# Prefix-sum diagonal on one core: more groups summed over rows by VectorE before TensorE, one row more per strip for ScalarE

## The chip, the core and the metric

The kernel runs on one core of a Trainium2 chip. A core has TensorE (PE, matrix products into PSUM), VectorE (DVE), ScalarE (ACT), GpSimd (POOL), SyncE (SP), and 16 DMA engines that bring data from the device memory to the on-chip memory of 128 partitions. The metric is device time in microseconds (us): 667.77 us, the median of 3 runs (667.74 to 668.14). One further execution was recorded by the profiler; the trace is of that one.

## What is computed

The input is x, four matrices of 4224 x 4224 float32 values (285 MB). For each matrix the result is the running sum along the diagonal of its two-dimensional prefix sums:

```python
ps = np.cumsum(np.cumsum(x, axis=1), axis=2)
diag = np.diagonal(ps, axis1=1, axis2=2)
return np.cumsum(diag, axis=1).astype(np.float32)
```

The diagonal entry n is the sum of the square x[0..n, 0..n]. So step n of it adds column n down to row n (above and on the diagonal) and row n up to column n-1 (left of the diagonal). The kernel forms these two sums for every n, adds them, and scans twice.

## The kernel before

A batch (one matrix) is cut along rows into strips. A strip has 768 rows, held as 128 partitions of F2 = 6 consecutive rows each, all 4224 columns wide, converted to bf16 by the DMA. There are NS = 5 such strips (s = 0 to 4) and then one of F = 3 rows per partition (384 rows). Columns are counted in NG = 11 groups of GW = 384. The last batch has four strips of 768 rows (s = 0 to 3), then one tile filled by two half-strip transfers of three rows per partition each (called the first and second half here), and the last 128 rows of the matrix are a tail of their own with `part_a` and `part_b`.

Three buffers hold strips (`NBUF` = 3). Strip DMAs are issued by POOL in program order (`load_rows`, line 75). The first three are issued at the start; each later one waits until everything that reads its buffer (the strip three places earlier) is done.

For each strip, `add_up` does the following.

- TensorE sums columns: for each group j to the right of the strip's own diagonal block, and for each of the six rows q, one matmul of 384 columns adds the strip into row j of `d`, an 11 x 384 accumulator in PSUM (`columns`; line 218 for the first of six, line 225 for the others).
- VectorE splits the diagonal block: `mu` is the block times an upper-triangular mask (line 353), and `mu` is subtracted from the block in place (line 354).
- In the first three batches, for strips s > 0, VectorE also adds the six rows of one group, the one just right of the block, into `rowed` (`row_sums`, line 267). TensorE then needs one fp32 matmul (run as two instructions) for this group in place of six.
- TensorE adds `mu` to `d`, two groups of six matmuls, and then `rowed`.
- The row sums left of the diagonal: ScalarE sums rows 0 to fs-1 of each partition, one activation with an accumulator per row (`act_sum`, line 262); VectorE sums the remaining rows in one reduction (line 267, `acc`). For 768-row strips fs = F = 3, so three rows each. Both read columns 0 to `hi`, the end of the strip's block: 768, 1536, 2304, 3072 and 3840 columns for s = 0 to 4.

After the strips of a batch VectorE copies the row sums to `r6` (line 400), TensorE adds them to `d`, VectorE makes sums of `d` (`pu`), TensorE forms the carries between groups, and VectorE scans twice (line 479).

Each engine works through its own instructions in program order. In the last batch this order is, for VectorE: strip s = 3 (`mu`, subtraction, `acc`), the two copies of line 400, the first half of the half strips (`mu`, subtraction, one row sum of 3456 columns), the second half, the fold of `fold_g`, the last row sums, `pu`, the scans, and the pair sums of the tail. For TensorE: the columns and `mu` of s = 3, six matmuls and three `mu` matmuls of the first half, 28 matmuls into a scratch tile called `ready` whose result is not used, 12 matmuls of `fold_g` over the second half (these use the PSUM buffer of `ready`), six more of the second half, the additions of the row sums to `d`, the folds `fold_part(0)` and `(1)`, the carries, and the tail with `fin_a`, `fin_b`, `fin_e`. The result `ye` is copied by VectorE and sent by SP as the last transfer.

The small pools matter for the order: `mu` and `rowed` come from `mup`, which has one buffer per name, so that each is written again only after TensorE has read it.

Of the kernel before, what the change touches and what calls it, by code (L numbers as in the profile page):

```python
# [8 lines left out]
FP32 = mybir.dt.float32  # L9
# [4 lines left out]
ACT = mybir.ActivationFunctionType  # L14
# [3 lines left out]
def kernel(  # L18
# [14 lines left out]
    nc = tc.nc  # L33
# [3 lines left out]
    P = 128  # L37
    F = 3
    F2 = 2 * F
    GW = P * F  # L40
    NG = N // GW
# [9 lines left out]
    mup = ctx.enter_context(tc.tile_pool(name="mup", bufs=1))  # L51
# [18 lines left out]
    def strip_tile():  # L70
        return strips.tile([P, F2, N], BF16, name="strip")

    def load_rows(o, b, r0):
        f = o.shape[1]
        nc.gpsimd.dma_start(  # L75
            out=o, in_=x[b, r0 : r0 + f * P, :].rearrange("(p f) w -> p f w", f=f)
        )
# [16 lines left out]
    sel = consts.tile([P, 2 * NG - 1], BF16, name="sel")  # L94
# [3 lines left out]
    def upper_mask(f):  # L98

        um = consts.tile([P, f, f * P], BF16, name=f"um{f}")  # L100
        nc.vector.memset(um, 1.0)  # L101
        nc.gpsimd.affine_select(  # L102
            out=um,
            in_=um,
            compare_op=ALU.is_gt,
            fill=0.0,
            base=0,
            pattern=[[-1, f], [1, f * P]],
            channel_multiplier=-f,
        )  # L110
        return um

    sel_f = consts.tile([P, 2 * NG - 1], FP32, name="sel_f")
    nc.vector.tensor_copy(out=sel_f, in_=sel)

    um6 = upper_mask(F2)
    um3 = upper_mask(F)
# [3 lines left out]
        out=um1,  # L121
        in_=um1,
# [10 lines left out]
        out=ident,  # L133
        in_=ident,
# [32 lines left out]
    def between_groups(name, turned):  # L167
# [27 lines left out]
        out=weights,  # L195
        in_=weights,
# [12 lines left out]
        out=steps, in_=steps, scalar=2, op=ALU.arith_shift_right  # L209
# [7 lines left out]
    def matmul(o, lhsT, rhs, start=False):  # L217
        nc.tensor.matmul(  # L218
            o, lhsT=lhsT, rhs=rhs, start=start, stop=False, skip_group_check=True
        )  # L220
# [36 lines left out]
    def act_sum(acc, src, own=None):  # L257
        w = src.shape[-1]
        dump = own
        if dump is None:  # L260
            dump = src
        nc.scalar.activation(  # L262
            out=dump[:, :w], in_=src, func=ACT.Copy, accum_out=acc
        )

    def row_sums(acc, src):
        nc.vector.reduce_sum(out=acc, in_=src, axis=AX.X)  # L267
# [18 lines left out]
    def masked(o, i, m, acc):  # L286
        nc.vector.scalar_tensor_tensor(  # L287
            out=o,
            in0=i,
            scalar=1.0,  # L290
            in1=m,
            op0=ALU.mult,
            op1=ALU.mult,
            accum_out=acc,
        )
# [21 lines left out]
    for b in range(B):  # L317
        whole = b < LB
        t0 = 0 if whole else 1
        r6, r3 = rows6[b % 2], rows3[b % 2]  # L320
        d = psum_d.tile([NG, GW], FP32, name="d")
# [6 lines left out]
        def row_of(j):  # L328
            return (j + t0) % NG

        def columns(j, lo, hi, rhs, same=False):


            k = row_of(j)
            lhsT = sel[:, NG - 1 - k : 2 * NG - 1 - k]
            if same:
                matmul_on(d[:, lo:hi], lhsT, rhs)
                return
            matmul(d[:, lo:hi], lhsT, rhs, start=first[0])
            first[0] = False  # L340

        def add_up(strip, f, r0, acc, um, fs=0, wp=0, ws=0, by_rows=False):


            nw = f * P // GW
            g = r0 // GW
            hi = r0 + f * P
            for j in range(g + nw + by_rows, NG):
                for q in range(f):
                    columns(j, 0, GW, strip[:, q, j * GW : (j + 1) * GW], q > 0)  # L350
            mu = mup.tile([P, f, f * P], BF16, name=f"mu{f}")
            block = strip[:, :, r0:hi]
            nc.vector.tensor_mul(out=mu, in0=block, in1=um)  # L353
            nc.vector.tensor_sub(out=block, in0=block, in1=mu)  # L354
            if by_rows:
                rowed = mup.tile([P, GW], FP32, name="rowed")
                row_sums(
                    rowed,
                    strip[:, :, hi : hi + GW].rearrange("p q c -> p c q"),
                )  # L360
            for h in range(nw):
                for q in range(f):
                    columns(g + h, 0, GW, mu[:, q, h * GW : (h + 1) * GW], q > 0)
            if by_rows:
                k = row_of(g + nw)
                matmul(d, sel_f[:, NG - 1 - k : 2 * NG - 1 - k], rowed)
            if fs:
                for q in range(fs):
                    act_sum(acc[:, q : q + 1], strip[:, q, :hi])
                row_sums(acc[:, fs:], strip[:, fs:, :hi])  # L370
            else:
                for q in range(f):
                    act_sum(acc[:, q, 0:1], strip[:, q, wp:ws])
                row_sums(acc[:, :, 1], strip[:, :, ws:hi])

        acc6 = smalls.tile([P, NS, F2], FP32, name="acc6")

        ns = NS if whole else NS - 1
        for s in range(ns):
            strip = prefetched.pop(0) if prefetched else None  # L380
            if strip is None:
                strip = strip_tile()
                load_rows(strip, b, s * F2 * P)
            add_up(
                strip, F2, s * F2 * P, acc6[:, s], um6, F, by_rows=whole and s > 0
            )
            if not whole and s == 0:
                diag_b = last.tile([P, P], BF16, name="diag_b")
                nc.gpsimd.dma_start(out=diag_b, in_=x[b, TB:N, TB:N])
            if not whole and s == 1:  # L390
                row_sums(hs[:, 2:3], diag_b)
                masked(hmu[:, 2, :P], diag_b, um1[:, :P], hu[:, 2:3])
                nc.vector.tensor_sub(out=dtot, in0=hs[:, 2:3], in1=hu[:, 2:3])
                for h in range(3):
                    columns(LG, h * P, GW, hmu[:, h, : GW - h * P], h > 0)
        a6 = acc6[:, :ns]
        for h in range(2):
            ps = slice(h * HP, (h + 1) * HP)
            k = row_of(h)
            nc.vector.tensor_copy(  # L400
                out=r6[ps, k : k + 2 * ns : 2, :], in_=a6[ps]
            )

        strip = strip_tile()
        if whole:
            load_rows(strip[:, :F], b, T0)
            add_up(strip[:, :F], F, T0, r3[:, LG], um3, F - 1)
        else:


            for h in range(2):
                load_rows(strip[:, h * F : h * F + F], b, T0 - (2 - h) * GW)
            add_up(strip[:, :F], F, T0 - 2 * GW, r3[:, row_of(LG - 2)], um3, F - 1)
            ready = psum_s.tile([P, 512], FP32, name="fold")
            for i in range(28):
                matmul(ready, ident_h, um6[:, i % F2, :512], start=True)
            fold_g = psum_s.tile([P, F, 160], FP32, name="fold")
            wp, ws = 1920, 1920 + 1248
            fold_in(fold_g, strip[:, F:], 0, wp, 160, start=True)
            parts = last.tile([P, F, 3], FP32, name="parts")  # L420
            add_up(strip[:, F:], F, T0 - GW, parts, um3, wp=wp, ws=ws)
            row_sums(parts[:, :, 2], fold_g)
            row_sums(r3[:, row_of(LG - 1), :], parts)

        if not whole:

            strip = strip_tile()
# [8 lines left out]
            for sb, c0, c1 in (  # L436
# [6 lines left out]
                r0 = TB + sb * R  # L443
                nc.gpsimd.dma_start(  # L444
                    out=part_b[:, sb, c0:c1],
                    in_=x[b, r0 : r0 + R, :TB].rearrange("r (k c) -> r k c", k=4)[
                        :, :, c0:c1
                    ],
# [3 lines left out]
            c0, c1 = acuts[0]  # L452
# [25 lines left out]
        for i, (to, src) in enumerate(((c1, d), (c2, c1))):  # L478
            nc.vector.tensor_tensor_scan(  # L479
                out=to,  # L480
# [29 lines left out]
        c0, c1 = acuts[1]  # L510
# [24 lines left out]
        for i in (1, 0):  # L535
# [5 lines left out]
            out=out[:LB, :].rearrange("b (g i) -> g b i", i=GW), in_=whole_sums  # L541
        )
        nc.sync.dma_start(
            out=out[b, :T0].rearrange("(g i) -> g i", i=GW), in_=last_sums[1:NG]
        )
        nc.sync.dma_start(
            out=out[b, T0 : T0 + M0].unsqueeze(0), in_=yl[:, :M0]
        )
        for i in (1, 0):
# [8 lines left out]
            out=out[b, T0 + M0 : T0 + E0].unsqueeze(0), in_=yl[:, M0:E0]  # L558
# [35 lines left out]
```

## Time and profile before

| | |
|---|---|
| median of 3 runs | 667.77 us (667.74 to 668.14) |
| profiled execution, its time | 667.48 us |
| profiled execution, span of the trace | 665.4 us |
| DMA queue of the strips, share of 16 engines | 99.9% (142.47 MB) |
| VectorE busy | 334.5 us (50%) |
| TensorE matmuls busy | 211.2 us (32%), 997 instructions |
| ScalarE busy | 154.5 us (23%) |
| GpSimd busy | 31.7 us (5%) |

The span is the time from the first to the last instruction on the core; 2.1 us of the execution's time lie around it. Times inside the trace are counted from the span's start. A line of the timeline gives start, duration, engine, source line, operation, output and inputs, and in brackets the idle time before it and what ended it. In the table of stretches, each engine's busy time and number of instructions are followed by the TensorE clock that was granted (1.00 is full speed, 0.50 half), the busy share of the DMA engines and their rate.

### The profile page before, as it was taken

The page shows a single profiled execution, that of the slowest core. Times are in us where ns is not written, and L with a number is a line of the kernel's source. Part 1 is how long each engine was busy: PE and PEld are TensorE (multiplying, and loading weights), DVE is VectorE, ACT ScalarE, POOL GpSimd, SP SyncE. Part 2 cuts the span into 40 slices and gives each one's busy share as a digit, 9 for nine tenths or more (in the row PEclk, how much of TensorE's full clock was granted, in tenths as well). Part 3 has the DMA queues.
Part 4 walks back from the last instruction along what each step waited for, and adds up shares of the span by engine and source line. Part 5 has one row for each costly group of instructions (what it writes and reads, how often), then busy time and mean ns, then how long its engine had stood idle before and what let it go on. Part 6 is the DMA issues. An engine that isn't in the chain of part 4 may idle for free.

```text
span 665.4 us, 2519 instructions
## 1 busy us (share of the span) xinstructions
PE 211.2 (32%) x997; PEld 97.2 (15%) x998; DVE 334.5 (50%) x160; ACT 154.5 (23%) x145; POOL 31.7 (5%) x60
## 2 busy tenths in 40 slices
PE   0071422303107143230311623404022253250458
PEld 0030210101103021010110311201001121120224
DVE  4141727466914163655782325456487323251746
ACT  0010203133511020322450102123154010221443
POOL 4200000000000000000000000000000000001000
PEclk9995857655558585665555957567565595765789
DMA  9999999999999999999999999999999999999998
GB/s 203 219 219 219 219 219 218 213 213 210 220 219 218 219 219 219 218 215 213 212 220 218 219 216 219 219 218 217 212 216 216 218 218 219 218 218 216 216 205 164
DMA packets 7666, 143.24 MB, mean 215 GB/s; under 512 B 698, under 2 KB 998, under 8 KB 2150
## 3 DMA queue, kind: packets, MB, share of 16 engines
q0 software_dynamic: 7312, 142.47, 99.9%
q1 hardware_dynamic: 342, 0.61, 0.3%
q8 instruction: 8, 0.13, 0.1%
q14 instruction: 4, 0.03, 0.0%
HBM read 285.47 MB, written 0.07 MB: 429 GB/s over the span
## 4 chain that ended last, share of the span: by engine, by line
DVE 42%; another core or an unknown queue 40%; DMA 11%; ACT 3%; issue 1%; PE 1%; POOL 1%; DVEq 0%; ACTq 0%; POOLq 0%
DVE acc L267 19%; DMA strip<-in_x_dram 11%; DVE mu L353 7%; DVE strip L354 7%; DVE rowed L267 7%; ACT strip L262 3%; PE d L218 0%; DVE c L479 0%; DVE whole_sums L479 0%; POOL strip L444 0%; DVE pu L267 0%; DVE whole_sums L287 0%; POOL strip L433 0%; DVE rows L400 0%
## 5 line engine op out<-in xcount | busy, mean ns | idle before, releaser
L262 ACT ACTIVATE strip<-strip 128x768 bf16<-128x768 bf16 (+9 forms) x71 | 150.3, 2118 | 481.7 <-DVE strip L354 450.8
L353 DVE TENSOR_TENSOR mu<-strip,um 128x4608 bf16<-128x4608 bf16 (+1 forms) x24 | 52.4, 2183 | 294.3 <-DMA strip<-in_x_dram 294.2
L225 PEld LDWEIGHTS <-sel 128*11 128x11 bf16 x643 | 66.5, 103 | 475.0 <-issue 445.1
L267 DVE TENSOR_REDUCE acc<-strip 128x3 f32<-128x2304 bf16 (+4 forms) x19 | 134.8, 7094 | 0.2
L218 PE MATMUL d<-strip,sel 128*11 128x384 bf16 x90 | 37.2, 413 | 286.9 <-DMA strip<-in_x_dram 286.9
L225 PE MATMUL d<-strip,sel 128*11 128x384 bf16 x441 | 115.6, 405 | 13.8 <-DMA strip<-in_x_dram 13.8
L354 DVE TENSOR_TENSOR strip<-strip,mu 128x4608 bf16<-128x4608 bf16 (+1 forms) x24 | 52.4, 2183 | 1.5
L267 DVE TENSOR_REDUCE rowed<-strip 128x384 f32<-128x2304 bf16 x12 | 49.3, 4110 | 0.0
L218 PE MATMUL d<-mu,sel 128*11 128x384 bf16 x43 | 15.9, 370 | 103.1 <-DVE mu L353 103.1
L225 PE MATMUL d<-mu,sel 128*11 128x384 bf16 x200 | 45.9, 364 | 0.0
L75 POOL DMA_DIRECT2D strip<-in_x_dram x23 | 15.7, 684 | 534.7 <-DVE acc L267 287.9
L218 PE MATMUL d<-rowed,sel_f 128*11 128x384 f32 x24 | 11.5, 568 | 21.9 <-DVE rowed L267 21.9
L267 DVE TENSOR_REDUCE rows<-strip 128x1 f32<-128x4224 bf16 (+1 forms) x4 | 17.4, 4353 | 0.1
L218 PEld LDWEIGHTS <-sel 128*11 128x11 bf16 x134 | 13.5, 101 | 22.7 <-issue 10.2
L262 ACT ACTIVATION_READ_ACCUMULATOR strip<-strip 128x1 f32 x71 | 13.2, 186 | 0.0
L218 PE MATMUL d<-ident,rows 128*11 128x128 f32 x24 | 5.7, 374 | 16.5 <-ACT strip L262 16.5
L267 DVE TENSOR_REDUCE pu<-d 11x1 f32<-11x384 f32 x4 | 2.2, 545 | 14.1 <-PE d L218 14.1
L218 PE MATMUL fold<-um,ident_h 128*128 128x512 bf16 x27 | 6.3, 392 | 0.3 <-issue 0.3
L262 ACT ACT_TABLE_LOAD x1 | 1.3, 1283 | 19.7 <-DMA strip<-in_x_dram 19.7
L102 POOL TENSOR_SCALAR_AFFINE_SELECT um<-um 128x4608 bf16<-128x4608 bf16 (+1 forms) x2 | 5.2, 2612 | 7.3 <-DVE um L101 7.3
L101 DVE MEMSET um<- 128x4608 bf16 (+1 forms) x2 | 4.9, 2458 | 1.1 <-issue 1.1
L218 PEld LDWEIGHTS d<-rowed,sel_f 128*11 128x11 f32 x24 | 1.5, 91 | 26.8 <-DVE rowed L267 26.4
(114 smaller groups left out, 75.8 us busy)
## 6 DMA issues: line engine op xcount, KB each, us to landing
strip<-in_x_dram POOLq DMA_DIRECT2D x18, 6336.0 KB, 73.5
strip<-in_x_dram POOLq DMA_DIRECT2D x7, 3168.0 KB, 57.5
strip<-in_x_dram POOLq DMA_DIRECT2D x1, 1080.0 KB, 51.6
strip<-in_x_dram POOLq DMA_DIRECT2D x1, 768.0 KB, 54.6
strip<-in_x_dram POOLq DMA_DIRECT2D x3, 256.0 KB, 55.9
head<-in_x_dram SPq DMA_DIRECT2D x1, 528.0 KB, 3.9
strip<-in_x_dram POOLq DMA_DIRECT2D x1, 192.0 KB, 43.2
strip<-in_x_dram POOLq DMA_DIRECT2D x1, 64.0 KB, 28.6
```

The source lines that it names most:

```text
L75: nc.gpsimd.dma_start(out=o, in_=x[b, r0 : r0 + f * P, :].rearrange("(p f) w -> p f w", f=f))
L101: nc.vector.memset(um, 1.0)
L102: nc.gpsimd.affine_select(out=um, in_=um, compare_op=ALU.is_gt, fill=0.0, base=0, pattern=[[-1, f], [1, f * P]], channel_multiplier=-f,)
L218: nc.tensor.matmul(o, lhsT=lhsT, rhs=rhs, start=start, stop=False, skip_group_check=True)
L225: te.add_instruction(mybir.InstMatmult(start_tensor_calc=False, stop_tensor_calc=False, tile_position=(0, 0), tile_size=(P, P if lhsT.shap ...
L262: nc.scalar.activation(out=dump[:, :w], in_=src, func=ACT.Copy, accum_out=acc)
L267: nc.vector.reduce_sum(out=acc, in_=src, axis=AX.X)
L353: nc.vector.tensor_mul(out=mu, in0=block, in1=um)
L354: nc.vector.tensor_sub(out=block, in0=block, in1=mu)
```

## The change

In every 768-row strip of all batches, two (s = 0) or three (other s) groups to the right of the block are first added over their six rows by VectorE, as far as there are that many: for s = 4 one group is left. Before it was one group, for s > 0, in the first three batches only. Each such group has a `rowed` buffer of its own. TensorE drops six bf16 matmuls per group and gets one fp32 matmul. ScalarE takes four of the six row sums to the left of the diagonal (F2 - 2) and VectorE two. A small constant, `sel_f`, is converted by ScalarE and no longer by VectorE.

```diff
     sel_f = consts.tile([P, 2 * NG - 1], FP32, name="sel_f")
-    nc.vector.tensor_copy(out=sel_f, in_=sel)
+    nc.scalar.activation(out=sel_f, in_=sel, func=ACT.Copy)
...
-        def add_up(strip, f, r0, acc, um, fs=0, wp=0, ws=0, by_rows=False):
+        def add_up(strip, f, r0, acc, um, fs=0, wp=0, ws=0, by_rows=0):
...
             block = strip[:, :, r0:hi]
             nc.vector.tensor_mul(out=mu, in0=block, in1=um)
             nc.vector.tensor_sub(out=block, in0=block, in1=mu)
-            if by_rows:
-                rowed = mup.tile([P, GW], FP32, name="rowed")
+            rowed = []
+            for i in range(by_rows):
+                rowed.append(mup.tile([P, GW], FP32, name=f"rowed{i}"))
+                c0 = hi + i * GW
                 row_sums(
-                    rowed,
-                    strip[:, :, hi : hi + GW].rearrange("p q c -> p c q"),
+                    rowed[i],
+                    strip[:, :, c0 : c0 + GW].rearrange("p q c -> p c q"),
                 )
             for h in range(nw):
                 for q in range(f):
                     columns(g + h, 0, GW, mu[:, q, h * GW : (h + 1) * GW], q > 0)
-            if by_rows:
-                k = row_of(g + nw)
-                matmul(d, sel_f[:, NG - 1 - k : 2 * NG - 1 - k], rowed)
+            for i in range(by_rows):
+                k = row_of(g + nw + i)
+                matmul(d, sel_f[:, NG - 1 - k : 2 * NG - 1 - k], rowed[i])
...
             add_up(
-                strip, F2, s * F2 * P, acc6[:, s], um6, F, by_rows=whole and s > 0
+                strip,
+                F2,
+                s * F2 * P,
+                acc6[:, s],
+                um6,
+                F2 - 2,
+                by_rows=min(2 if s == 0 else 3, NG - 2 * s - 2),
             )
```

## The prediction

> **What bounds the kernel now.** I read the page's busy table and its DMA lines first:
>
> ```profile
> PE 211.2 (32%) x997; PEld 97.2 (15%) x998; DVE 334.5 (50%) x160; ACT 154.5 (23%) x145; POOL 31.7 (5%) x60
> ...
> q0 software_dynamic: 7312, 142.47, 99.9%
> ```
>
> No engine is busy for more than half the span, while the strip queue keeps the 16 DMA engines busy for 99.9%. Then I cut the span at the times when strips land (where VectorE's `mu` of each begins):
>
> ```profile
> 34.59:64.54 29.95, 7.67 (x3) 0.77 1.01 217
> 64.54:95.19 30.65, 14.01 (x4) 0.67 0.99 212
> 125.14:155.09 29.95, 18.79 (x4) 0.61 1.01 217
> 589.05:618.90 29.85, 12.47 (x3) 0.61 1.01 217
> ```
>
> A 768-row strip takes 29.9 us whether VectorE works 7.7 or 18.8 us of it. Compute can only matter if it starves this queue, or after the last landings. The end of the chain that ended last shows the second:
>
> ```profile
> 619.15 43.18 DMA strip<-in_x_dram
> 662.35 0.41 DVE pair L276 x2
> 662.76 0.04 issue
> 662.81 0.48 PE fin_e L218 x6
> 663.29 0.02 issue
> 663.31 0.18 DVE ye L562
> ```
>
> The last piece lands at 662.35 and 1.0 us later the result is copied. The stretch before that, in the timeline:
>
> ```profile
> 624.21 9.75 DVE L267 TENSOR_REDUCE acc<-strip 128x3 f32<-128x9216 bf16 x1
> 634.07 0.36 DVE L400 COPY rows<-acc 64x24 f32<-64x24 f32 x2
> 634.46 0.76 DVE L353 TENSOR_TENSOR mu<-strip,um 128x1152 bf16<-128x1152 bf16 x1
> 636.04 3.75 DVE L267 TENSOR_REDUCE rows<-strip 128x1 f32<-128x3456 bf16 x1
> 637.23 6.31 PE L218 MATMUL fold<-um,ident_h 128*128 128x512 bf16 x27 [0.33 <-issue]
> 648.88 0.58 PE L218 MATMUL fold<-strip,ident_h 128*128 128x480 bf16 x1 [5.34 <-DMA strip<-in_x_dram]
> 648.93 0.76 DVE L353 TENSOR_TENSOR mu<-strip,um 128x1152 bf16<-128x1152 bf16 x1 [9.13 <-DMA strip<-in_x_dram]
> 657.66 0.38 PE L218 MATMUL fold_a<-strip,ident_h 128*128 128x512 bf16 x1 [0.29 <-DMA strip<-in_x_dram]
> ```
>
> Before the last half strip lands (648.88), VectorE has idled 9.1 us and TensorE 5.3 us. That idle time is what the change can use up.
>
> **The change, part by part.**
>
> *Whole-span sums.* The `rowed` reductions go from 12 to 47 (12 per whole batch, 11 in the last): 35 x 4.11 us = 144 us on VectorE. Two rows for three saves a third of the 134.8 us of `acc`, 45 us. Net 334.5 + 99 = 433 us, under the span. ScalarE gains 19 activations of 0.83 to 3.39 us, about 41 us. TensorE drops 210 bf16 matmuls and gains 70 fp32 ones.
>
> *Does the queue starve?* A strip's buffer comes free 3 x 4.03 us after the subtraction, not 1 x, less the saved row. VectorE's end moves, for s = 1, 2, 3 of a whole batch, by 8.1 less 1.6, 2.4 and 3.2 us (a third of 4.9, 7.3 and 9.7), so by 6.5 to 4.9 us later; s = 0 moves from 46.5 (TensorE) to 49.8. For s = 4 VectorE ends 4.0 us earlier; ScalarE, with four activations at 3.4 us, takes over the end at about 174.0, still earlier than 176.4. The tightest cover: the issue at 144.71 moves to 149.6, and its strip is next in line only at 170.1 (it lands at 200.1, less 29.9). So 20 us of queued transfers hide it, 25 us or more elsewhere. In the last batch (no `rowed` before, so 12.1 less 1.6 or 2.4 us) the issues of 570.0 and 602.4 move by about 10 us; their data are next at 618.9 and 648.9, 37 us later. All cost nothing. If such cover were gone, each us late would be a us of the span. POOL's issues keep their order. `sel_f`, 21 columns on ScalarE, is done before the first strip lands at 34.6.
>
> *The end of the last batch.* This is where the sum is made.
>
> 1. VectorE, s = 3: 624.21 + 3 x 4.03 + 6.5 (two thirds of 9.75) + 0.1 = 642.9; the copies end at 643.3. The `mu` of the first half starts at 643.3 in place of 634.46: 8.8 us late. It, the subtraction and the 3.75 us reduction end at 648.6, so VectorE is just free (0.3 us) for the last half. Its own delay is hidden; TensorE's is not.
> 2. TensorE, in order: the third `rowed` at 636.4 (1.3 us at half clock), six columns until 639.6, then idle until `mu` at 644.1. The three `mu` matmuls and the gap after them took 1.1 us (635.73 to 636.83), so `ready` begins at 645.2.
> 3. The 28 `ready` matmuls and the 12 of `fold_g` behind them depend on the granted clock. At half clock `fold_g` matmuls of 480 columns start every 0.40 us (weight loads at 649.26, 649.66, 650.06), so those of 512 every 0.427; at full clock it is half of that and a little more, 0.203 and 0.216 (`ready` before: 2.4 slow and 25.6 fast ones and 0.17 us of drain make its 6.7 us). The clock is at half after 4.4 us of idling, as in the trace:
>
> ```profile
> 624.00:626.00 2.00, 2.00 (x13) 0.95 1.06 228
> 637.00:638.00 1.00, 0.77 (x3) 0.57 1.24 270
> 648.00:649.00 1.00, 0.12 (x1) 0.55 1.01 203
> 651.00:652.00 1.00, 1.00 (x6) 0.74 1.06 216
> ```
>
> The means place the rises at 624.2, 637.9 and 651.5: 5.3, 4.0 and 2.6 us after the first matmul (618.90, 633.86, 648.88). With the middle one the clock rises at 648.1: 2.9 us of half clock make 6.8 matmuls, 21.2 more take 4.6 us, and with 0.17 us of drain `ready` ends at 652.85. `fold_g` starts at 652.9, not 648.88, but runs at full clock: 12 x 0.203 = 2.4 us, so the next matmul is at 655.35 instead of 652.70. **2.65 us late.**
> 4. ScalarE is no later: the two 3.08 us rows after 645.0, then the three short ones, end at 655.0, before `fold_g` is reduced.
> 5. The additions to `d`, `pu`, carries and scans follow one another and keep the 2.65 us: the last scan ends at 662.1. Two TensorE waits for DMA (0.29 before 657.66, 0.45 before 659.07) vanish, and the one idle bit before `fin_a` shrinks, so `fin_a` starts at 662.95 (before 660.47). From there TensorE needs 1.9 us to the end of the `bsum` matmuls (before 662.40), 664.9, and `fin_e` follows at once where it waited before for the last pair sum. `ye` is copied at 665.35 instead of 663.31: **2.05 us late.**
>
> With the rise after 2.6 us `ready` ends 0.7 us earlier, after 5.3 us 0.65 us later: 1.4 and 2.7 us. I take the middle row. Sum: 667.48 + 2.05 = **669.5 us**. The profiled execution is 0.29 us under the median of 667.77, which is within the runs' spread (0.40).
>
> The Trainium skill, TensorE: Matmul & The Clock Gate, Part 1, says that the clock is released after a busy window of about 3.4 us, that the windows run freely, and that an idle window takes it back. By it the rise after 644.1 comes 3.4 to 6.8 us later and the end is 1.8 to 3.4 us late, 669.3 to 670.9. The trace disagrees at the short side, where 2.6 us were enough; so a window seems not to need to be busy throughout.
>
> *Costs that the trace does not show.* `rowed` over the second and third group: bound by its own row, 4.08 to 4.18 us each, and by an `acc` of the same 2304 elements, 2.55; I take 4.03 from start to start, as the order of columns is `rowed`'s. A two-row `acc`: between one row (3.75 for 3456 columns) and three (9.75). DMA per strip: 29.85 to 30.65 us; I take no change.
>
> **The rivals.**
>
> *The clock is already full at 644.1.* The new burst of 636.4 to 639.6 might wake it; the clock also stayed full for 4.6 us after a last matmul (643.5 to 648.1), and here 4.4 pass. Against: the burst lasts 3.2 us and the rises took 2.6 to 5.3, and elsewhere the clock fell sooner (at 50.8 after matmuls that end at 47.9). Then `ready` ends at 651.4, `fold_g` follows at full clock, the next matmul comes at 653.9, 1.2 us late, and the end, which returns 0.6 as above, 0.6 us late: 668.1.
>
> *VectorE overruns the last half too.* Its margin is 0.3 us. If `rowed` took 4.6 us beside four ScalarE rows, the first `mu` and all behind it would be 1.7 us later still, and the last `mu` 1.4 us late: 671.2. It decides from 4.13 us on, where the margin is gone (3 x 0.1). Against: 4.08 to 4.18 in all 12.
>
> *Other side: faster.* With less TensorE traffic transfers could run faster. The span is 22 strip times long, and to come out 1.3 us under the median in spite of the late end each would have to shrink by 0.14 us (3.1 us in all); intervals do differ by up to 0.8 us (30.65 and 29.85). At 0.2 us each, 4.4 us: 665.1. Against: 29.95 with TensorE busy for 13.28 us (34.59 to 64.54) and for 6.90 us (125.14 to 155.09) alike.
>
> *The tail hides all* (`ready` never holds up the half strip): 667.5. Against: TensorE's order above.
>
> **How the numbers follow.** A measurement of this kernel can tell about 0.2% (1.3 us) from no change: 666.4 to 669.1 counts as same. The forecast gets 0.74, range 668.8 to 670.3; 0.09 of it lies under 669.1. The clock rival 0.10 (same), the overrun 0.06 (slower), the hidden tail 0.03 (same), faster transfers 0.07. So slower 0.71, same 0.22, faster 0.07. The range reaches to the hidden tail and towards the overrun: 667.4 to 670.8.
>
> **What would show it.** After: strips still land every 29.9 us and the last piece near 662.4; `rowed` x47 at 4.1 us; the first half's `mu` near 643.3; `ready` ending near 652.9 and the first `fold_g` matmul after it, no longer released by DMA; `ye` near 665.3. The prediction is wrong if strip intervals change, if a `mu` waits for something other than its landing in mid-batch, or if `fold_g` still starts at 648.9.

## The result, and the profile after

The changed kernel takes 669.15 us in the median of 22 runs (668.20 to 670.70), the kernel before 667.82 us in 22 runs beside it (667.37 to 668.86). The ratio is 1.0019, with a 95% interval of 1.0013 to 1.0025: slower by 1.3 us. The loss is clear of zero. It lies at the bound of 0.2% that the prediction set for "no change", which the interval includes. The profiled execution took 668.88 us, with a span of 667.2 us; before it was 667.48 and 665.4.

The first lines of the page after:

```profile
PE 222.5 (33%) x858; PEld 82.7 (12%) x858; DVE 428.7 (64%) x194; ACT 193.2 (29%) x184; POOL 31.7 (5%) x60
...
q0 software_dynamic: 7312, 142.47, 99.7%
...
L267 DVE TENSOR_REDUCE rowed<-strip 128x384 f32<-128x2304 bf16 x47 | 189.2, 4078 | 0.0
```

VectorE works 94 us more (prediction: 99), and the strip queue is as full as it was. TensorE has 139 matmul records fewer and is nevertheless "busy" for longer, because the bf16 matmuls that are left run more often at half clock (those on `mu` take 412 ns in the mean, before 364) and the added fp32 ones are slow (705 ns mean). Neither sum says anything about the end time here.

Cutting the span after the change at the landings of strips (columns: stretch, its length, VectorE's busy time and instructions, granted clock, DMA share, GB/s):

```profile
34.62:64.58 29.96, 14.77 (x5) 0.77 1.01 217
64.58:95.42 30.84, 20.32 (x7) 0.67 0.99 212
125.31:155.25 29.94, 23.59 (x7) 0.56 1.01 217
589.12:618.99 29.87, 21.94 (x6) 0.61 1.01 217
```

VectorE's share of these stretches has grown from 7.7 to 14.8 us and from 18.8 to 23.6 us, but the landings keep their distance. The strip s = 3 of the last batch lands at 618.99; before it was 618.95. Up to this point nothing is lost.

The timeline after, from there on, as VectorE and TensorE show it:

```profile
624.13 12.09 DVE L267 TENSOR_REDUCE rowed<-strip 128x384 f32<-128x2304 bf16 x3
636.12 6.56 DVE L267 TENSOR_REDUCE acc<-strip 128x2 f32<-128x6144 bf16 x1
643.17 0.76 DVE L353 TENSOR_TENSOR mu<-strip,um 128x1152 bf16<-128x1152 bf16 x1
648.95 0.76 DVE L353 TENSOR_TENSOR mu<-strip,um 128x1152 bf16<-128x1152 bf16 x1 [0.44 <-DMA strip<-in_x_dram]
655.41 0.66 DVE L267 TENSOR_REDUCE parts<-fold 128x3 f32<-128x480 f32 x1 [2.62 <-PE fold L225]
664.96 0.18 DVE L570 COPY ye<-fin_e 1x32 f32<-1x32 f32 x1 [0.31 <-PE fin_e L218]
```

```profile
643.98 0.48 PE L218 MATMUL d<-mu,sel 128*11 128x384 bf16 x1 [4.34 <-DVE mu L353]
645.03 7.70 PE L218 MATMUL fold<-um,ident_h 128*128 128x512 bf16 x28
652.78 0.36 PE L218 MATMUL fold<-strip,ident_h 128*128 128x480 bf16 x1
655.30 0.33 PE L218 MATMUL d<-strip,sel 128*11 128x384 bf16 x1
```

VectorE itself is in time for the last half strip: it starts at its landing (648.95) after 0.44 us of idling. TensorE is not. Its first `fold_g` matmul has lost the bracket that named the DMA before. It follows the 28 `ready` matmuls directly, 3.9 us after the landing, and VectorE then waits 2.6 us for it. The chain that ended last no longer runs through the last transfer. It goes back through TensorE's `ready` to VectorE's `rowed`:

```profile
624.21 12.00 DVE rowed L267 x3
636.22 6.47 DVE acc L267
642.78 0.17 DVE rows L408
642.96 0.18 DVE rows L408
643.17 0.77 DVE mu L353
643.98 0.48 PE d L218
644.46 0.64 PE d L225 x2
645.10 7.65 PE fold L218 x28
```

### The profile page after: what moved, and what is told of

The parts are those of the page before. It is cut to its first block, busy times and chain, and to the rows that moved or that the text cites. A ratio compares the mean times of both kernels' runs of the same rounds, so it can differ in the third digit from the quotient of the medians.

```text
span 667.2 us, 2307 instructions
## 1 busy us (share of the span) xinstructions
PE 222.5 (33%) x858; PEld 82.7 (12%) x858; DVE 428.7 (64%) x194; ACT 193.2 (29%) x184; POOL 31.7 (5%) x60
## 4 chain that ended last, share of the span: by engine, by line
DVE 54%; another core or an unknown queue 27%; ACT 10%; DMA 5%; PE 3%; issue 1%; POOL 0%; DVEq 0%; ACTq 0%; POOLq 0%
DVE rowed L267 26%; DVE acc L267 10%; ACT strip L262 10%; DVE mu L353 8%; DVE strip L354 8%; DMA strip<-in_x_dram 5%; PE fold L218 1%; PE d L218 1%; DVE c L487 1%; DVE whole_sums L487 0%; PE fold L225 0%; DVE pu L267 0%; DVE whole_sums L287 0%; DVE rows L408 0%
## 5 line engine op out<-in xcount | busy, mean ns | idle before, releaser
L262 ACT ACTIVATE strip<-strip 128x768 bf16<-128x768 bf16 (+8 forms) x90 | 189.0, 2101 | 458.9 <-DVE strip L354 458.9
L267 DVE TENSOR_REDUCE rowed<-strip 128x384 f32<-128x2304 bf16 x47 | 189.2, 4078 | 0.0
L225 PEld LDWEIGHTS <-sel 128*11 128x11 bf16 x468 | 50.7, 108 | 374.2 <-issue 357.0
L218 PE MATMUL d<-rowed,sel_f 128*11 128x384 f32 x94 | 57.3, 705 | 109.3 <-DVE rowed L267 109.3
L267 DVE TENSOR_REDUCE acc<-strip 128x2 f32<-128x1536 bf16 (+4 forms) x19 | 90.8, 4777 | 0.0
L218 PE MATMUL d<-strip,sel 128*11 128x384 bf16 x55 | 23.5, 428 | 167.3 <-DMA strip<-in_x_dram 167.3
L225 PE MATMUL d<-strip,sel 128*11 128x384 bf16 x266 | 73.5, 421 | 13.8 <-DMA strip<-in_x_dram 13.8
L218 PE MATMUL d<-mu,sel 128*11 128x384 bf16 x43 | 17.8, 414 | 130.1 <-DVE mu L353 130.1
L225 PE MATMUL d<-mu,sel 128*11 128x384 bf16 x200 | 53.9, 412 | 0.0
L218 PEld LDWEIGHTS d<-rowed,sel_f 128*11 128x11 f32 x94 | 5.4, 95 | 147.0 <-DVE rowed L267 146.4
L262 ACT ACTIVATION_READ_ACCUMULATOR strip<-strip 128x1 f32 x90 | 16.8, 187 | 0.0
L218 PEld LDWEIGHTS <-sel 128*11 128x11 bf16 x99 | 10.8, 109 | 26.1 <-issue 16.7
L218 PE MATMUL d<-halves,rows 128*11 128x64 f32 x48 | 5.3, 289 | 0.0
```

The lines of the kernel that those rows point to most:

```text
L218: nc.tensor.matmul(o, lhsT=lhsT, rhs=rhs, start=start, stop=False, skip_group_check=True)
L225: te.add_instruction(mybir.InstMatmult(start_tensor_calc=False, stop_tensor_calc=False, tile_position=(0, 0), tile_size=(P, P if lhsT.shap ...
L262: nc.scalar.activation(out=dump[:, :w], in_=src, func=ACT.Copy, accum_out=acc)
```

## Experiments

The theory was that all of the loss arises in this end of the last batch, by TensorE's queue. The main rivals were a loss spread over the batches, a lateness of VectorE and ScalarE themselves, and a clock that is missing when the last half strip lands.

### The one strip undone, and the one strip alone

Undone, from the changed kernel:

```diff
-                by_rows=min(2 if s == 0 else 3, NG - 2 * s - 2),
+                by_rows=0 if not whole and s == 3 else min(2 if s == 0 else 3, NG - 2 * s - 2),
```

> The changed kernel, but strip s = 3 of the last batch has no rowed groups (TensorE adds its three groups column by column, as before); the other 44 rowed groups and ScalarE's fourth row stay. Theory A (the time was lost only in the last batch's end: the first half strip's mu 8.7 us late, and ready and fold_g behind it on TensorE): the first half's mu is back near 631, fold_g starts with the landing at 648.9, ye near 663.3, time as the kernel before, 667.8 (ratio 0.9995 to 1.0005). Rival B (the 1.3 us are spread over the batches: VectorE's 100 us more, later buffers): at least two thirds of the loss stays, 668.7 to 669.1.

Measured: 667.43 us (667.20 to 668.16, 10 runs), ratio 0.9994 (0.9985 to 1.0003). The loss is gone, although 44 of 47 `rowed` groups are still there. The first half's `mu` came at 636.10, not near 631 as expected. The half strip had landed before that, as TensorE's first matmul on it shows (634.17); `mu` had to wait behind VectorE's copies of the row sums, and these waited 4.62 us for ScalarE's fourth row. In this variant the fourth row thus holds up VectorE, which the expectation had left out. It costs nothing, as `fold_g` is released by its DMA again:

```profile
634.17 0.48 PE L218 MATMUL d<-strip,sel 128*11 128x384 bf16 x1 [8.04 <-DMA strip<-in_x_dram]
635.71 0.36 DVE L408 COPY rows<-acc 64x24 f32<-64x24 f32 x2 [4.62 <-ACT strip L262]
636.10 0.76 DVE L353 TENSOR_TENSOR mu<-strip,um 128x1152 bf16<-128x1152 bf16 x1
649.15 0.38 PE L218 MATMUL fold<-strip,ident_h 128*128 128x480 bf16 x1 [3.92 <-DMA strip<-in_x_dram]
663.62 0.18 DVE L570 COPY ye<-fin_e 1x32 f32<-1x32 f32 x1 [0.31 <-PE fin_e L218]
```

Alone, with all other strips as before:

```diff
-                F2 - 2,
-                by_rows=min(2 if s == 0 else 3, NG - 2 * s - 2),
+                F2 - 2 if not whole and s == 3 else F,
+                by_rows=3 if not whole and s == 3 else int(whole and s > 0),
```

> The other way round: all strips as before the change, and only strip s = 3 of the last batch gets its three rowed groups and ScalarE's fourth row. Theory A: 669.1 (ratio 1.0015 to 1.0025), ye near 665.0. Rival B: no more than 668.2, as 44 of 47 rowed groups and most of VectorE's added work are gone.

Measured: 669.30 us (668.37 to 670.35, 10 runs), ratio 1.0022 (1.0013 to 1.0032). One of the 19 strips of 768 rows brings the whole loss. The two together rule out a loss spread over the batches.

### What in that strip's wake is late

The `ready` matmuls write a scratch tile that nobody reads. Their number was cut to 10 in the changed kernel:

```diff
-            for i in range(28):
+            for i in range(10):
                 matmul(ready, ident_h, um6[:, i % F2, :512], start=True)
```

> The changed kernel with 10 scratch matmuls in ready instead of 28; their result is not used. Theory A1 (TensorE's backlog of ready matmuls is what is late): ready ends near 648.7 (at 645.0, seven at half clock and three at full), fold_g starts with the landing at 648.95 at full clock, ye near 663.4, time 667.6 to 667.9. Rival A2 (VectorE's and ScalarE's own lateness carries the delay: ScalarE's short rows end at 654.8 in place of 652.65): the row sums stay late, 668.7 to 669.2. Rival A3 (without ready the clock stays at half through fold_g): next matmul near 653.8, time 668.2.

> The changed kernel with 10 scratch matmuls in ready once more, with more rounds: ratio to the kernel before 0.9990 (0.9985 to 0.9995). If the first result was chance: 1.0000.

Measured: 667.24 us (667.09 to 667.75, 10 runs), ratio 0.9989 (0.9979 to 0.9998), and again 667.27 us (667.08 to 667.55, 11 runs), ratio 0.9989 (0.9980 to 0.9998). The first theory's expectation, 667.6 to 667.9, was nearest; why the time is lower still is taken up below. VectorE's `mu` is as late as in the changed kernel, yet the loss is gone:

```profile
643.14 0.76 DVE L353 TENSOR_TENSOR mu<-strip,um 128x1152 bf16<-128x1152 bf16 x1
645.40 3.21 PE L218 MATMUL fold<-um,ident_h 128*128 128x512 bf16 x9 [0.33 <-issue]
648.87 0.38 PE L218 MATMUL fold<-strip,ident_h 128*128 128x480 bf16 x1 [0.26 <-DMA strip<-in_x_dram]
654.81 0.16 DVE L267 TENSOR_REDUCE rows<-parts 128x3 f32<-128x9 f32 x1 [1.49 <-ACT strip L262]
663.33 0.18 DVE L570 COPY ye<-fin_e 1x32 f32<-1x32 f32 x1 [0.31 <-PE fin_e L218]
```

So the late `mu` does its harm only through the `ready` matmuls queued behind it. ScalarE's lateness is visible too: the `parts` reduction waits 1.49 us for its rows. But its delay of 1.2 us (654.81 against 653.57) is within what the end can absorb: `ye` is copied at 663.33, before the change at 663.31. There is little left to absorb with, for the chain that ended last now runs through `acc`, `mu` and ScalarE's rows and no longer through a transfer.

Without `ready` altogether (the tile and the loop taken out of the changed kernel):

> The changed kernel without ready. TensorE idles from 645.0 to 648.9 after three short matmuls, so fold_g runs at half clock at first. If only TensorE's backlog made the change slow, this is at 667.4 to 667.9, as the kernel before and 0.2 to 0.6 us over the variant with 10. If the clock at the landing were what the change lost, it would be 668.5 or more.

Measured: 667.28 us (667.03 to 668.11, 10 runs), ratio 0.9991 (0.9982 to 1.0000). In its profile 11 of the `fold_g` matmuls take 4.60 us at half clock instead of the 2.39 of the changed kernel:

```profile
649.65 4.60 PE L225 MATMUL fold<-strip,ident_h 128*128 128x480 bf16 x11
```

The chain that ended last runs through them. This execution was the slowest of the ten (668.11 us), so the half clock may well cost something where it occurs; in the median nothing of it is seen.

### How much VectorE time the end can hold

Two groups instead of three in that one strip:

```diff
-                by_rows=min(2 if s == 0 else 3, NG - 2 * s - 2),
+                by_rows=min(2 if s == 0 or not whole and s == 3 else 3, NG - 2 * s - 2),
```

> The changed kernel with two rowed groups, not three, in the last batch's s = 3; all else stays. Theory A1 (TensorE's backlog decides, with a threshold): the first half's mu at 639.2, ready from 640.3 to about 648.3, still before the landing at 648.9, so nothing is lost: 667.3 to 667.6. A theory in which each group costs its share (4 us of VectorE each, a third of the loss): 668.7.

Measured: 667.69 us (667.17 to 668.52, 10 runs), ratio 0.9997 (0.9988 to 1.0006). The cost has a threshold and is not a third per group: two thirds of the loss would have been 668.7. In its profile the `mu` is at 639.78, but `ready` does not end near 648.3 as expected. The clock rose late, and `fold_g` starts at 650.26, 0.7 us after the landing of that execution:

```profile
642.04 8.16 PE L218 MATMUL fold<-um,ident_h 128*128 128x512 bf16 x27 [0.33 <-issue]
650.26 0.36 PE L218 MATMUL fold<-strip,ident_h 128*128 128x480 bf16 x1
```

The end absorbs this, and the chain ends with the last transfer again. The time lies just over the expected 667.3 to 667.6; whether the second group costs a few tenths of a us, these runs can't tell.

More VectorE time in the same place: ScalarE back to three rows, in the changed kernel.

```diff
-                F2 - 2,
+                F,
```

> The changed kernel with ScalarE summing three rows as before, so that VectorE's acc in the last s = 3 takes 9.75 us instead of 6.5. If VectorE's time before the first half's mu sets the end: mu at 646.4, VectorE busy past the last landing by 2.9 us, ready from 648.3 on, fold_g at about 656, end 5 us later than before: 672 to 673. If ScalarE's fourth row were a cost and not a help: 669 or less.

Measured: 672.17 us (672.00 to 673.48, 4 runs), ratio 1.0068 (1.0053 to 1.0083). VectorE now runs past the last landing, and `fold_g` starts 3.0 us later than in the changed kernel:

```profile
646.36 0.76 DVE L353 TENSOR_TENSOR mu<-strip,um 128x1152 bf16<-128x1152 bf16 x1
651.61 0.75 DVE L353 TENSOR_TENSOR mu<-strip,um 128x1152 bf16<-128x1152 bf16 x1
655.77 0.36 PE L218 MATMUL fold<-strip,ident_h 128*128 128x480 bf16 x1
```

ScalarE's fourth row thus earns 3 us next to the other half of the change; the half with `rowed` alone, which is this run, is slower by 4.4 us (672.17 against 667.77). In this one step a us on VectorE is about a us at the end (3.2 us later `mu`, 3.0 us longer).

### VectorE's work in the middle of a batch

In the variant with 10 scratch matmuls, the first two groups of every strip of the whole batches were reduced twice, the second time over the first:

```diff
-                row_sums(
-                    rowed[i],
-                    strip[:, :, c0 : c0 + GW].rearrange("p q c -> p c q"),
-                )
+                for _ in range(2 if whole and i < 2 else 1):
+                    row_sums(
+                        rowed[i],
+                        strip[:, :, c0 : c0 + GW].rearrange("p q c -> p c q"),
+                    )
```

> The changed kernel with 10 scratch matmuls, and in the whole batches the first two rowed groups of every strip are computed twice (27 more reductions of 4.0 us, 108 us of VectorE; each is overwritten by the same sums). If the queued transfers hide VectorE's work in mid-batch (the tightest cover falls from 20 to 12 us), strips land every 29.9 us still and the time is as with 10 scratch matmuls, 667.3 (ratio 0.9985 to 0.9995). If VectorE's work slows the transfers or lets the queue run dry: 669 or more.

Measured: 667.16 us (667.00 to 667.36, 10 runs), ratio 0.9989 (0.9979 to 0.9998). VectorE is busy for 537.1 us, 81% of the span, and works 29.73 of 29.90 us between two landings:

```profile
PE 225.8 (34%) x839; PEld 81.0 (12%) x840; DVE 537.1 (81%) x221; ACT 193.4 (29%) x184; POOL 31.7 (5%) x60
```

```profile
125.30:155.20 29.90, 29.73 (x9) 0.50 1.01 217
289.70:319.60 29.90, 29.73 (x9) 0.56 1.01 217
```

Neither the transfers nor the buffers mind.

### Where the 0.5 us under the kernel before come from

The variants without the loss (10 scratch matmuls, none, reduced twice) are not level with the kernel before but 0.5 to 0.6 us under it. A first idea was the clock at the last landing: before, it has fallen to half there. The kernel before, with `range(46)` in place of `range(28)`, so that TensorE works on until the landing:

> The kernel before with 46 scratch matmuls in ready instead of 28, so that TensorE works until about 648 and the last half strip lands on a full clock. If the 0.5 us by which the variant with 10 scratch matmuls beat the kernel before come from the clock at that landing (before, it falls to half in the 5.3 us of idling, and how soon it rises differs from run to run): 667.2 to 667.4, with less spread, ratio 0.9988 to 0.9995. If they come from the changed row sums: 667.8, as the kernel before.

Measured: 667.77 us (667.62 to 668.44, 10 runs), ratio 1.0001 (0.9992 to 1.0010). Its profile shows `fold_g` at full clock from the landing on, and the time doesn't move:

```profile
648.87 0.38 PE L218 MATMUL fold<-strip,ident_h 128*128 128x480 bf16 x1 [0.42 <-DMA strip<-in_x_dram]
649.09 2.39 PE L225 MATMUL fold<-strip,ident_h 128*128 128x480 bf16 x11
```

This idea fell.

Splitting each run's time into span and rest shows where the difference lies, partly. The rest is 2.04 to 2.07 us in the median for the kernel before, and 1.70 to 1.72 us for the changed kernel and the variants with 10 or no scratch matmuls. (Where `fold_g` is late, single executions have a longer rest: up to 2.79 us in the changed kernel. Why is open.) Two more runs asked whether the small `sel_f` conversion does this. First the kernel before with this line alone changed:

```diff
-    nc.vector.tensor_copy(out=sel_f, in_=sel)
+    nc.scalar.activation(out=sel_f, in_=sel, func=ACT.Copy)
```

> The kernel before with nothing but sel_f converted by ScalarE. In the runs so far the time less the span is 2.05 us in the median for the kernel before and for it with 46 scratch matmuls, and 1.7 to 1.8 for all that have the changed sel_f. If the moved conversion (ScalarE's table load at 0.8 us in place of 19.7) is the cause: time less span 1.7, time 667.4, span as before. If the shorter TensorE program is the cause: 2.05 and 667.8.

Measured: 667.69 us (667.41 to 669.76, 12 runs), ratio 0.9999 (0.9989 to 1.0009); rest 1.85 us against 2.07 beside it. Then the reverse edit in the variant with 10 scratch matmuls:

> The changed kernel with 10 scratch matmuls and sel_f back on VectorE. If sel_f is the cause of the smaller time outside the span: 2.05 outside, 667.6 in all. If the shorter TensorE program is the cause: 1.7 outside, 667.25 as with sel_f on ScalarE.

Measured: 667.56 us (667.25 to 668.71, 12 runs), ratio 0.9995 (0.9986 to 1.0004); rest 1.72 us. So `sel_f` shortens the rest by 0.2 us in one kernel and by nothing in the other, where the TensorE program is shorter. Neither explanation holds alone, and what fills this time outside the span stays open. So does the other part of the gain, some 0.2 us of span (665.5 to 665.6 in the median with 10 scratch matmuls or none, against 665.7 to 665.8 beside them; with `sel_f` back on VectorE it is 665.85 against 665.9).

## Why the prediction was right, point by point

- **Bound by the transfers; mid-batch costs nothing.** Right. Landings stayed 29.9 us apart, the issue that was put at 149.6 came at 149.53, and 108 us more on VectorE changed nothing. The cover of 20 us was worked out from the queue and was not used up by any run, so its exact size isn't shown.
- **Step 1, VectorE in the last s = 3.** Right to 0.13 us: `mu` at 643.17 (643.3 was said), and the margin before the last half strip was 0.44 us (0.3 said). The run with three ScalarE rows shows the margin from the other side.
- **Steps 2 and 3, TensorE, `ready` and the clock.** Right: `ready` from 645.03 (645.2), the first `fold_g` matmul at 652.78 (652.9), the one after `fold_g` at 655.30 (655.35). The choice of the middle of three rows for the clock's rise, at 648.1, was met by this execution; that is in part luck, as the next paragraph shows. In stretches of TensorE alone (length, busy time and instructions, granted clock, DMA share, GB/s) the clock is at half until 648:

```profile
647.00:648.00 1.00, 1.00 (x4) 0.50 0.58 120
648.00:649.00 1.00, 1.00 (x6) 0.97 0.98 194
```

  The rise differs from execution to execution. Here it comes 4.1 us after the first `mu` matmul (643.98). With only this strip changed it came after 3.6 us (mean clock 0.84 from 647 to 648, first `mu` matmul at 643.74), with three ScalarE rows after 3.7 (0.57 from 650 to 651; 647.17), and with two groups after 5.8 (0.78 from 646 to 647; 640.60), which is more than the longest of the three rows. In the variant with only this strip changed `fold_g` starts at 652.30 and `ye` is at 664.48, both 0.48 us earlier than in the changed kernel; half of this is an earlier `mu` (0.24 us), the other half is left for the clock. A wider scatter fits this: the middle half of the runs spans 1.2 us after and 0.4 us before. That the clock makes all of the scatter wasn't tested, and in part it lies outside the span (the rest is 1.66 to 2.79 us).
- **The rule on the clock.** The Trainium skill, TensorE: Matmul & The Clock Gate, Part 1, says that the clock is released after a busy window of about 3.4 us. The trace agrees: the rise came 4.1 us after the `mu` matmuls began, within the 3.4 to 6.8 us that the prediction estimated from this rule, as are the 3.6, 3.7 and 5.8 us above. The 669.3 to 670.9 us worked out from it, though, lie above the measured 669.15, because of two terms that are told below (the way to the end, and the sum).
- **Step 4, ScalarE is no later than `fold_g`.** Right: the wait for its rows shows only where `ready` was cut (1.49 us, until 654.81).
- **Step 5, the way to the end.** Right in kind, with one term too large. The last scan ends at 662.03 (662.1 said) and `fin_a` starts at 662.87 (662.95). From there to the last `fin_e` matmuls the prediction took the 1.9 us from before; measured are 1.66 us (662.87 to 664.53). The 1.9 us had contained two short waits, for a pair sum and for one of ScalarE's row sums (0.07 us before 661.97, 0.09 before 662.17), and both sums are now done in time. The other 0.1 us is that the prediction counted to the end of the last `bsum` matmul, where the next one starts before it ends. With all this `ye` is 1.65 us late (664.96 against 663.31), not 2.05.
- **The sum.** It counted the time around the span as unchanged (2.1 us). It was 1.7 us. This is the second term that was mis-sized, the one that no step had. In the medians the span went from 665.8 (the kernel before, in the runs beside the experiments) to 667.4, up 1.6, and the rest down by 0.33: 1.3 us of net loss, where 1.7 to 2.05 was forecast. Why the rest fell is open, as said above.
- **The chances.** Slower by over 0.2% was held likeliest (0.71); the ratio, 1.0019, is just under this bound, so that the measured case counts as "same" (0.22). Within it, it is the one of the forecast's own mechanism at the low end of its range (0.09). The time of 669.15 us lies within that range (668.8 to 670.3).
- **The rivals.** The clock was not full at 643.98: the first `ready` matmuls run at half. It was close, though: in the profile of the variant with 10 scratch matmuls and `sel_f` on VectorE, the burst that ends at 639.9 did wake the clock (mean 0.86 from 640 to 641), and it fell back only at about 643.85 (mean 0.85 from 643 to 644), 0.3 us before the first `mu` matmul there. VectorE did not overrun: `rowed` took 4.08 us in the mean and at most 4.15, the new columns among them. The transfers were not faster. The end did not hide it all.

## What to carry to other kernels

In this kernel, whose transfers fill the span, VectorE time in mid-batch was free up to 81% busy. The same work in the last strip before the end was free only up to a threshold: two groups cost nothing clear of the noise, the third group made the loss, and in the one step measured beyond that a us cost about a us. A change that is applied "in every strip" is to be judged in the last one first. An engine that is in time itself can still make another late, through what that one has queued behind the late input. Matmuls that only keep a clock up are worth a second look whenever what stands ahead of them moves: here 28 of them became 3.9 us of delay, and with 10 of them the changed kernel is about 0.1% faster than the kernel before (667.24 and 667.27 us against 667.77 and 667.82), a gain whose cause is open.

## What the hardware showed that was not expected

- The `ready` matmuls, which are there to keep TensorE's clock up, earn nothing that the medians show: without them the changed kernel takes 667.28 us, with 10 of them 667.24 and 667.27. In the kernel before, 46 of them give 667.77 against 667.82 with 28; it was not run with fewer.
- The time outside the span is not a constant: in the median it is 2.04 to 2.07 us with the kernel before, 1.85 with `sel_f` on ScalarE alone, and 1.70 to 1.72 with the changed kernel and its variants with 10 or no scratch matmuls. The 0.33 us between the first and the last gave back a fifth of the 1.6 us by which the late end lengthened the span.
- An fp32 matmul of the `rowed` kind costs as much TensorE time as four bf16 ones of the same 384 columns. At half clock its two instructions run from 636.27 until the next matmul starts at 637.52, 1.25 us, while bf16 ones start every 0.32 us (637.52, 637.84):

```profile
636.27 1.45 PE L218 MATMUL d<-rowed,sel_f 128*11 128x384 f32 x2 [2.54 <-DVE rowed L267]
637.52 0.52 PE L218 MATMUL d<-strip,sel 128*11 128x384 bf16 x1
637.84 0.84 PE L225 MATMUL d<-strip,sel 128*11 128x384 bf16 x2
```

  One `rowed` group thus saves TensorE two matmuls of six, for 4 us of VectorE.
